# Which engines split the down projection's weights: ScalarE and the Pool in place of the Pool and VectorE

## The chip, the cores and the metric

The kernel runs on one core of one Trainium2 chip. The metric is the device time of one execution in microseconds (us). The profile names the engines PE (TensorE matmul), PEld (TensorE weight load), DVE (VectorE), ACT (ScalarE), POOL (GpSimd) and SP (the engine that issues the DMAs).

## The reference

A two-layer backbone over 1024 latent tokens and 256 context tokens of width 1024, in float32. Layer 0 mixes with chunked gMLP gating beside a bidirectional gated DeltaNet, layer 1 with latent attention; both end in a ConvFFN, which is where the change lies:

```python
def conv_ffn(h, w_up, conv_w, w_down):
    g, u = jnp.split(dwconv(h @ w_up, conv_w), 2, axis=-1)
    return (jax.nn.silu(g) * u) @ w_down

lat = lat + g2 * conv_ffn(modulate(rms_norm(lat, norm2_g[i]), sh2, sc2), ffn_w_up[i], ffn_conv_w[i], ffn_w_down[i])
```

The hidden width is 2816, so `w_down` is 2816 x 1024. Layer 0 runs the ConvFFN over latent and context tokens (1280), layer 1 over the latent ones (1024). A final RMSNorm follows.

## The kernel before, in words

Activations lie transposed: features on the 128 partitions, tokens along the free dimension. Every large product is done in three matmuls on float32r operands. Each operand is split in two halves: `hi` is the value cast to float32r, `lo` is the value minus `hi`, and the product is `hi*hi + hi*lo + lo*hi`. The helper `split(hi, lo, src, eng)` (L130) does this with one cast (`cast`, L119 to L128) and one subtraction (L133); `eng` chooses the engines. With `"pool"` the Pool casts (L126) and DVE subtracts; with `"act"` ACT casts (L124) and DVE subtracts; with `"pools"` the Pool does both.

A ConvFFN has two passes. `ffn_up` multiplies by `w_up`, convolves along the tokens, gates, and stores the 22 hidden tiles in DRAM. `ffn_down` (L544), the second pass, multiplies by `w_down`. It goes over chunks of tokens: in layer 0 one of 512 columns and three of 256, in layer 1 one of 512 and two of 256. For each chunk it computes the output in two halves of four 128-row tiles (`oh`), each half in four PSUM banks. A half needs 11 weight tiles of 128 x 1024 (`wdr`, 512 KB each), so a chunk needs 22, and the tiles are loaded and split anew in every chunk: 22 x 4 + 22 x 3 = 154 times. One weight tile feeds a group of 24 matmuls (L633 with `wdh` and the activation's upper half `ah`, L634 with `wdh` and `al`, L635 with `wdl` and `ah`).

The order of work is kept three tiles deep. After group i is issued, `weight(i + 2)` splits the tile two groups ahead, and `load(i + 3)` asks SP for the raw tile three groups ahead. There are three raw buffers and three pairs of split buffers, so the split of tile i + 2 has to wait until PE has finished group i - 1, and the load of tile i + 3 until the split of tile i has read its raw buffer. `fetch` and `halve` bring the hidden tiles of later groups from DRAM and split them with ACT and DVE (`ah`, `al`). After each half, DVE adds the four PSUM banks, times a gate, onto the residual `x` (L650).

Beside the groups runs the `tail` of a chunk: squares on ACT and the Pool (L206, L208), their sums by matmul (`nsum` L196, `nall` L217), the inverse root on ACT and DVE (L219 to L230), and then in layer 0 the modulation of the eight tiles of the next mixer's input (L249 to L254, two tiles on the Pool by `affine`, L236, six on DVE and ACT) and in layer 1 the final norm (L2128 to L2131). The first steps of a tail run in the chunk's second half, the rest in the first half of the chunk after.

Each engine runs its own queue in order. What goes first in a queue is set by the framework's planner, which orders the instructions by its own model of time when the kernel is built; buffers and semaphores are placed by it as well.

Of the kernel before, what the change touches and what calls it, by code (L numbers as in the profile page):

```python
# [10 lines left out]
ALU = mybir.AluOpType  # L11
# [38 lines left out]
def f(ap):  # L50
    return ap.bitcast(F32)
# [46 lines left out]
class Kern:  # L98
# [30 lines left out]

    def split(self, hi, lo, src, eng):  # L130

        self.cast("pool" if eng == "pools" else eng, hi, src)
        (self.nc.gpsimd if eng == "pools" else self.nc.vector).tensor_tensor(lo, src, f(hi), ALU.subtract)  # L133

    def mm3(self, ps, ws, xs, first=True, last=True):

# [407 lines left out]
    def ffn_down(self, l, wp, chunks, groups, tile_x, x, g2, tail, early=None):  # L544
# [7 lines left out]
        raws, W, A, X = {}, {}, {}, {}  # L552

        def load(i):
            if i < total and i not in raws:
                raws[i] = wp.tile([P, KD, P], F32, tag="wur", name="wdr", bufs=3)
                nc.sync.dma_start(raws[i], self.I["w_down"][l, i // npr % 2, i % npr])

        def weight(i):
            load(i)  # L560
            if i < total and i not in W:

                p, bufs = (wp, 2) if i % 3 < 2 else (self.ffz, 1)
                W[i] = [p.tile([P, KD, P], F32R, tag="wu" + a, name="wd" + a, bufs=bufs) for a in "hl"]
                self.split(*W[i], raws[i], "pool")

        def fetch(ch, gi):

# [35 lines left out]
        def run():  # L604
            load(0)
            weight(0)
            load(1)
            fetch(0, 0)
            fetch(0, 1)
            yield  # L610
            weight(1)
            load(2)
            halve(0, 0)
            halve(0, 1)
            yield
            weight(2)
            load(3)
            todo = sequence()
# [1616 lines left out]
```

## Time and profile before

| what | value |
|---|---|
| time, median of 3 runs | 3243.54 us (3239.95 to 3248.44) |
| time of the profiled execution | 3249.41 us |
| its span | 3247.3 us |
| second pass in layer 0 | about 1452 to 1796 us of the span |
| second pass in layer 1 | about 2970 to 3234 us of the span |
| PE / DVE / POOL / ACT busy | 96% / 67% / 40% / 34% |
| casts of `wdr`, Pool | 154, 189.3 us |
| subtractions for `wdl`, DVE | 154, 199.4 us |

A row of the groups view names the line, engine, operation, what is written and read, the shape and the count; behind the bar stand the busy time and the mean of one in ns; behind the second bar stand the idle time of that engine just before these instructions and what ended most of it. A row of the waits view says who waited for whom, with total, times and the longest, in us. A row of the timeline has the start, the duration, the engine, the line and, in brackets, the idle time ahead of it. A row of the windows view has a stretch of the span, its length, and each engine's busy time with the number of instructions, then the granted PE clock, the DMA engines' share and GB/s. A line can be a helper's: L126 and L133 are the cast and the subtraction of every user of `split`, which is why the tile's name matters.

### The profile page before, as it was taken

Reading aid. Unit: us, or ns where it says so; the run is one execution under the profiler, and the core shown is the slowest. Engines: PE = TensorE matmul, PEld = TensorE weight load, DVE = VectorE, ACT = ScalarE, POOL = GpSimd, SP = SyncE. Lnnn points to the kernel's source line nnn. Section 1 sums busy time; section 2 is a strip of 40 time slices with the busy share of each in tenths; the row PEclk is TensorE's granted clock in tenths of the full one; section 3 lists DMA queues with packets and bytes.
Section 4 is the critical chain, followed back from the end, with each engine's and each line's share of the span. In section 5 each row is a group of like instructions: output and inputs, shape, how many; then the busy total and the mean of one; then the engine's idle time right before and its main releaser. Section 6 shows DMA issues by size and latency. Waiting matters only on the chain. (4 is left out here: it accounts for less than half of the span.)

```text
span 3247.3 us, 48696 instructions
## 1 busy us (share of the span) xinstructions
PE 3106.5 (96%) x19029; PEld 2599.4 (80%) x19029; DVE 2167.6 (67%) x3218; ACT 1105.0 (34%) x2136; POOL 1305.6 (40%) x1181
## 2 busy tenths in 40 slices
PE   7999899998999999999999999999999899999998
PEld 5767777896777788887889778988978787777888
DVE  6333877566875578884477456666666888888455
ACT  5322233333432233340111255555542333333110
POOL 3244323553443354532345232122133566663243
PEclk9999999999999999999999999999999899999999
DMA  7344957753144521244466231000033122225464
GB/s 253 124 140 125 303 144 214 229 171 117 40 141 150 162 97 68 70 154 167 137 222 222 72 110 44 27 22 22 8 117 124 46 78 78 78 79 200 165 198 150
DMA packets 254436, 411.40 MB, mean 127 GB/s; under 512 B 46576, under 2 KB 163520, under 8 KB 254080
## 3 DMA queue, kind: packets, MB, share of 16 engines
q1 hardware_dynamic: 254208, 408.31, 39.3%
q8 instruction: 150, 2.46, 0.3%
q14 instruction: 78, 0.64, 0.1%
HBM read 327.47 MB, written 80.78 MB: 126 GB/s over the span
## 5 line engine op out<-in xcount | busy, mean ns | idle before, releaser
L635 PE MATMUL dn<-ah,wdl 128*128 128x256 f32 (+1 forms) x1232 | 385.1, 318 | 15.4 <-DVE wdl L133 15.4
L633 PE MATMUL dn<-ah,wdh 128*128 128x256 f32 (+1 forms) x1232 | 389.5, 317 | 5.0 <-DVE x L650 4.3
L634 PE MATMUL dn<-al,wdh 128*128 128x256 f32 (+1 forms) x1232 | 387.2, 315 | 0.0
L126 POOL TENSOR_SCALAR wdh<-wdr 128x1024 fp32r<-128x1024 f32 x154 | 189.3, 1230 | 358.4 <-PE dn L634 233.0
L133 DVE TENSOR_TENSOR wdl<-wdr,wdh 128x1024 fp32r<-128x1024 f32 x154 | 199.4, 1301 | 176.3 <-POOL wdh L126 174.2
L635 PEld LDWEIGHTS dn<-ah,wdl 128*128 128x128 f32 x1232 | 234.1, 192 | 34.8 <-DVE wdl L133 18.5
L633 PEld LDWEIGHTS dn<-ah,wdh 128*128 128x128 f32 x1232 | 235.9, 191 | 27.8 <-issue 5.1
L634 PEld LDWEIGHTS dn<-al,wdh 128*128 128x128 f32 x1232 | 235.8, 191 | 15.2
L133 DVE TENSOR_TENSOR wul<-wur,wuh 128x1024 fp32r<-128x1024 f32 x106 | 163.3, 1541 | 97.5 <-POOL wuh L126 97.5
L126 POOL TENSOR_SCALAR wuh<-wur 128x1024 fp32r<-128x1024 f32 x106 | 137.0, 1293 | 222.5 <-PE upc L409 111.6
L1721 POOL TENSOR_SCALAR p<-p,rsm 128x1280 f32<-128x1280 f32 x63 | 84.7, 1345 | 325.9 <-DVE rsm L1714 177.0
L675 DVE SCALAR_TENSOR_TENSOR y<-raw,fconv,y 128x1023 f32<-128x1023 f32 (+1 forms) x132 | 174.1, 1347 | 31.6 <-ACT y L420 31.2
L140 PE MATMUL proj<-hh,wih 128*128 128x512 f32 (+1 forms) x512 | 183.8, 361 | 0.0
L677 DVE SCALAR_TENSOR_TENSOR y<-raw,fconv,y 128x1023 f32<-128x1023 f32 (+1 forms) x132 | 180.1, 1386 | 0.1
L141 PE MATMUL proj<-hl,wih 128*128 128x512 f32 (+1 forms) x512 | 177.8, 348 | 1.0 <-DVE hl L254 1.0
L142 PE MATMUL proj<-hh,wil 128*128 128x512 f32 (+1 forms) x512 | 177.1, 346 | 1.1 <-DVE wil L133 1.1
L427 POOL TENSOR_TENSOR y<-y,y 128x1280 f32<-128x1280 f32 (+1 forms) x42 | 119.8, 2853 | 108.1 <-issue 62.7
L393 POOL TENSOR_TENSOR s<-wur 128x512 f32<-128x512 f32 x42 | 72.7, 1731 | 184.4 <-DMA wur<-in_w_up 129.3
L1703 DVE TENSOR_REDUCE mx<-sc 128x1 f32<-128x512 f32 (+1 forms) x192 | 114.5, 597 | 39.9 <-PE sc L1702 37.9
L420 ACT ACTIVATE y<-raw,fconv 128x1280 f32<-128x1280 f32 (+1 forms) x88 | 110.6, 1259 | 82.0 <-DVE raw L436 75.6
L111 ACT ACTIVATE p<-sc,nmx 128x512 f32<-128x512 f32 (+1 forms) x192 | 116.2, 617 | 49.4 <-DVE nmx L1707 49.2
L124 ACT ACTIVATE ah<-al 128x512 fp32r<-128x512 f32 (+1 forms) x77 | 52.4, 744 | 185.2 <-DMA al<-act 174.9
(544 smaller groups left out, 9351.9 us busy)
## 6 DMA issues: line engine op xcount, KB each, us to landing
wdr<-in_w_down SPq DMA_DIRECT2D x154, 512.0 KB, 3.9
adaw<-in_ada_w SPq DMA_DIRECT2D x96, 512.0 KB, 4.2
wur<-in_w_up SPq DMA_DIRECT2D x88, 512.0 KB, 3.6
al<-act SPq DMA_DIRECT2D x20, 1024.0 KB, 7.6
t<-t SPq DMA_DIRECT2D x20, 768.0 KB, 6.6
act<-y SPq DMA_DIRECT2D x22, 640.0 KB, 3.0
act<-y SPq DMA_DIRECT2D x22, 512.0 KB, 2.6
wir<-in_w_t SPq DMA_DIRECT2D x20, 512.0 KB, 4.6
```

The lines of the kernel that those rows point to most:

```text
L111: self.nc.scalar.activation(out, in_, func, **kw)
L126: nc.gpsimd.tensor_scalar(dst, src, 1.0, 0.0, op0=ALU.mult, op1=ALU.add)
L133: (self.nc.gpsimd if eng == "pools" else self.nc.vector).tensor_tensor(lo, src, f(hi), ALU.subtract)
L140: nc.tensor.matmul(ps, wh, xh, start=first and i == 0, stop=False)
L141: nc.tensor.matmul(ps, wh, xl, start=False, stop=False)
L142: nc.tensor.matmul(ps, wl, xh, start=False, stop=last and i == n - 1)
L427: (nc.gpsimd if ci < FT - 1 else nc.vector).tensor_tensor(y[1], y[0], y[1], ALU.mult)
L633: nc.tensor.matmul(pss[o], wh[:, q, :], ah, start=pr == j == 0, stop=False)
L634: nc.tensor.matmul(pss[o], wh[:, q, :], al, start=False, stop=False)
L635: nc.tensor.matmul(pss[o], wl[:, q, :], ah, start=False, stop=pr == npr - 1 and j == 1)
L675: nc.vector.scalar_tensor_tensor(out=y[:, s0 + 1:e], in0=raw[:, s0:e - 1], scalar=w[:, 0:1], in1=y[:, s0 + 1:e], op0=ALU.mult, op1=ALU.add)
L677: nc.vector.scalar_tensor_tensor(out=y[:, s0:e - 1], in0=raw[:, s0 + 1:e], scalar=w[:, 2:3], in1=y[:, s0:e - 1], op0=ALU.mult, op1=ALU.add)
```

## The change

`split` takes an engine name that may end in "s". The name without it chooses the engine of the cast; the "s" says that the Pool subtracts, and otherwise DVE does. `"pool"`, `"act"` and `"pools"` mean what they meant. `ffn_down` now asks for `"acts"`: for each of the 154 weight tiles ACT casts and the Pool subtracts. The loads, the matmuls, the buffers and everything outside of `weight` are written as before.

```diff
     def split(self, hi, lo, src, eng):
 
-        self.cast("pool" if eng == "pools" else eng, hi, src)
-        (self.nc.gpsimd if eng == "pools" else self.nc.vector).tensor_tensor(lo, src, f(hi), ALU.subtract)
+        self.cast(eng.rstrip("s"), hi, src)
+        (self.nc.gpsimd if eng[-1] == "s" else self.nc.vector).tensor_tensor(lo, src, f(hi), ALU.subtract)
...
                 W[i] = [p.tile([P, KD, P], F32R, tag="wu" + a, name="wd" + a, bufs=bufs) for a in "hl"]
-                self.split(*W[i], raws[i], "pool")
+                self.split(*W[i], raws[i], "acts")
```

## The prediction

> **What bounds the kernel now.** I read the page first: its head, its engine shares and the groups that hold the edited instructions.
>
> ```profile
> span 3247.3 us, 48696 instructions
> PE 3106.5 (96%) x19029; PEld 2599.4 (80%) x19029; DVE 2167.6 (67%) x3218; ACT 1105.0 (34%) x2136; POOL 1305.6 (40%) x1181
> ...
> L635 PE MATMUL dn<-ah,wdl 128*128 128x256 f32 (+1 forms) x1232 | 385.1, 318 | 15.4 <-DVE wdl L133 15.4
> L633 PE MATMUL dn<-ah,wdh 128*128 128x256 f32 (+1 forms) x1232 | 389.5, 317 | 5.0 <-DVE x L650 4.3
> ...
> L126 POOL TENSOR_SCALAR wdh<-wdr 128x1024 fp32r<-128x1024 f32 x154 | 189.3, 1230 | 358.4 <-PE dn L634 233.0
> L133 DVE TENSOR_TENSOR wdl<-wdr,wdh 128x1024 fp32r<-128x1024 f32 x154 | 199.4, 1301 | 176.3 <-POOL wdh L126 174.2
> ```
>
> TensorE (PE) is busy 96% of the span. The edited work, 154 casts and 154 subtractions, is never on its path except where a matmul waits for a weight's lower half: 15.4 us in the whole run. Another 4.3 us are waits for the PSUM evictions (L650), which stand in VectorE's (DVE) queue beside those subtractions. So the most that this change can win is 15.4 + 4.3 = 19.7 us, 0.6%. The waits by layer (first row the first ConvFFN, second row the second one) show where:
>
> ```profile
> PE dn L635 <- DVE wdl L133: 12.4, 10, 2.7
> ...
> PE dn L635 <- DVE wdl L133: 3.0, 1, 3.0
> ```
>
> Next I read the rhythm where nothing disturbs it, in the timeline of the second ConvFFN (256-column chunk):
>
> ```profile
> 3152.05 1.06 POOL L126 TENSOR_SCALAR wdh<-wdr 128x1024 fp32r<-128x1024 f32 x1 [1.79 <-PE dn L634]
> 3154.90 1.06 POOL L126 TENSOR_SCALAR wdh<-wdr 128x1024 fp32r<-128x1024 f32 x1 [1.78 <-PE dn L634]
> ...
> 3153.15 1.23 DVE L133 TENSOR_TENSOR wdl<-wdr,wdh 128x1024 fp32r<-128x1024 f32 x1 [1.63 <-POOL wdh L126]
> ```
>
> One weight comes every 2.85 us, which is one group of 24 matmuls. A cast starts when PE leaves the buffer, two groups (5.7 us) before the weight is needed; it takes 1.06, and the subtraction ends at 3154.38, 2.3 us after the start. So 5.7 - 2.3 = 3.4 us are to spare. At 512 columns a group is about twice as long, and nothing there is near the limit.
>
> Then the chunks of 256 columns, one stretch each (three in the first ConvFFN, two in the second):
>
> ```profile
> core 0: us, PE busy (x) PEld busy (x) DVE busy (x) ACT busy (x) POOL busy (x), PEclk, DMA share, GB/s
> 1582.00:1658.00 76.00, 68.46 (x540) 64.61 (x539) 53.33 (x50) 15.98 (x26) 37.10 (x29) 0.98 0.63 211
> 1658.00:1728.00 70.00, 66.06 (x544) 63.72 (x544) 54.57 (x59) 13.65 (x28) 37.40 (x31) 1.00 0.67 216
> 1728.00:1796.00 68.00, 67.07 (x558) 65.38 (x557) 48.38 (x54) 9.15 (x20) 36.64 (x31) 1.00 0.65 208
> ...
> 3093.00:3171.00 78.00, 72.48 (x560) 68.53 (x559) 48.95 (x48) 9.03 (x16) 33.10 (x28) 0.93 0.60 193
> 3171.00:3234.00 63.00, 62.98 (x536) 61.50 (x538) 35.05 (x36) 4.74 (x12) 25.32 (x24) 1.00 0.54 162
> ```
>
> 22 groups of 2.85 would be 62.7 us; four of the five take 68 to 78. There the previous chunk's norm and modulation run beside the groups, DVE is 63 to 78% busy and ACT 12 to 21%.
>
> **What the Pool and DVE do to each other.** These rows are the start of such a burst, and the same DVE pair a little later:
>
> ```profile
> 1609.03 2.21 POOL L249 TENSOR_TENSOR t<-x,t 128x512 f32<-128x512 f32 x1 [0.62 <-DVE t L230]
> 1611.20 1.50 POOL L126 TENSOR_SCALAR wdh<-wdr 128x1024 fp32r<-128x1024 f32 x1
> ...
> 1610.01 3.23 DVE L252 SCALAR_TENSOR_TENSOR t<-x,gs,t 128x512 f32<-128x512 f32 x2
> 1627.94 1.40 DVE L252 SCALAR_TENSOR_TENSOR t<-x,gs,t 128x512 f32<-128x512 f32 x2
> ```
>
> Two DVE instructions with two SBUF inputs take 1.40 us in one place and 3.23 beside Pool work, and the Pool's cast goes from 1.06 to 1.50. They take turns. So I count the time in which either holds the other off: per weight now 1.06 + 1.23 = 2.29 us.
>
> **The change, part by part.** Removed: 154 Pool casts (189.3 us) and 154 DVE subtractions (199.4 us). Added: 154 ScalarE (ACT) casts and 154 Pool subtractions of the same shape. The rows nearest to them:
>
> ```profile
> L124 ACT ACTIVATE ah<-al 128x1024 fp32r<-128x1024 f32 x22 | 22.1, 1052 | 66.7 <-DMA al<-act 66.7
> ...
> L133 POOL TENSOR_TENSOR wkl<-wur,wkh x4: 2438/2806/2842, 2397.0 to 2410.3; 128x1024 fp32r<-128x1024 f32 x4
> ...
> 2397.02 8.37 POOL L133 TENSOR_TENSOR wkl<-wur,wkh 128x1024 fp32r<-128x1024 f32 x3
> 2410.35 2.44 POOL L133 TENSOR_TENSOR wkl<-wur,wkh 128x1024 fp32r<-128x1024 f32 x1
> ...
> L133 DVE TENSOR_TENSOR ol<-o,oh x24: 407/553/2868, 2393.9 to 2417.0; 128x256 fp32r<-128x256 f32 x16, 128x512 fp32r<-128x512 f32 x8
> ```
>
> The cast is the very same instruction form on ACT: 1.05 us each, 162 us in all. The subtraction is the same form on the Pool: 2.44 us at best, 2.81 when DVE's two-input work (ol, up to 2.87 us instead of some 0.6) alternates with it. I take 2.44 for most and 2.81 inside bursts, 154 times, 376 to 432 us against 189 now.
>
> The Trainium skill, "SBUF — State Buffer", section "SBUF: two separate sides", calls the pair of ports that DVE and GpSimd share an exclusive lock held for the whole instruction; the rows above agree (ol 2.87 us beside wkl). "Perfetto Trace Analysis", section "Optimizing Scalar/DVE Operations", draws from it that moving work between these two engines might not help: by that rule alone the sum would be 0, and mine differs only by waits with other causes.
>
> Held time per weight becomes 2.44, against 2.29: the casts leave the contest, the subtraction comes back twice as long. So a burst that is limited by the two engines taking turns stays as long as it is, and I win nothing of the waits inside bursts. What changes is who queues:
>
> (a) DVE's queue gets 22 x 1.3 = 29 us shorter per chunk. Of the 4.3 us of eviction waits about half stood behind subtractions: -2 (bounds -4.3 and 0).
>
> (b) Two waits have a cause that the change removes.
>
> ```profile
> 1456.31 1.18 POOL L126 TENSOR_SCALAR wdh<-wdr 128x1024 fp32r<-128x1024 f32 x1 [4.34 <-issue]
> ...
> 1464.34 1.21 DVE L133 TENSOR_TENSOR wdl<-wdr,wdh 128x1024 fp32r<-128x1024 f32 x1
> ...
> 3124.51 5.54 POOL L2129 TENSOR_TENSOR x<-x,t 128x512 f32<-128x512 f32 x3 [0.68 <-DVE t L230]
> 3130.02 4.39 POOL L126 TENSOR_SCALAR wdh<-wdr 128x1024 fp32r<-128x1024 f32 x3
> ```
>
> At the start of the first ConvFFN's second pass a cast ended at 1457.5 and its subtraction came at 1464.34, behind conv taps on DVE; the Pool is free there: -2 of that wait of up to 2.7 (0 at worst, as activations' halves stay on DVE). At 3124 three Pool products held up the casts for 5.5 us and PE then stood 3.0 us; the cast now goes on ACT meanwhile, and the subtraction ends near 3130.0 + 2.4 = 3132.5 instead of after 3135: -3.
>
> (c) Each weight is ready later: 1.05 + 2.44 = 3.5 us after release instead of 2.3, spare 5.7 - 3.5 = 2.2. Undisturbed chunks hide that. In a burst whose spare is used up, it costs 1.2 us once; the ten waits of the first ConvFFN fall into about five bursts: +5 (0 if the freed DVE catches up, +12 if each wait pays).
>
> (d) The raw weight's buffer comes free by the subtraction, so its reload is issued 1.2 us later.
>
> ```profile
> SPq L557 <- DVE wdl L133: 254.2, 83, 8.5
> ...
> POOL wdh L126 <- DMA wdr<-in_w_down: 48.7, 24, 5.5
> ```
>
> Loads wait for the subtraction 83 times, and 24 casts already waited for a load. Most are hidden by the spare; I charge one, +1 (up to +4 for the longest stretch).
>
> (e) ACT's 162 us lie in an engine that is 34% busy: nothing, unless its order is bad (third rival). Behind a cast that waits for PE's release stand ACT's squares, Ln/Exp and halvings, which have groups of time.
>
> Sum: -2 - 2 - 3 + 5 + 1 = -1 us. The profiled execution took 3249.4 us (span 3247.3 and 2.1 around it), 5.9 above the median of the runs, so its own figure would be 3248; against the median 3243.5 I forecast 3243. Adding the worst and best of the terms gives -9.3 (-4.3 - 2 - 3) to +13 (-3 + 12 + 4), 3234 to 3257 with no burst cured.
>
> **The rivals.**
>
> First, faster: DVE's queue, not the turn-taking, is the cause of the waits. For it: DVE is the busiest engine after PE in the bursts, and in the row at 1464.34 the subtraction alone is late. Against it: held time per weight doesn't fall. It would take nearly all of the 19.7 us away, say 18: 3225.
>
> Second, slower: the Pool becomes the bound of the 256-column chunks. In the first three of them its work beside the weights is
>
> ```profile
> L126 POOL TENSOR_SCALAR wdh<-wdr 128x1024 fp32r<-128x1024 f32 x64 | 84.8, 1327 | 87.9 <-DMA wdr<-in_w_down 38.8 <-PE dn L634 29.7 <-DVE al L133 6.4
> ```
>
> 37.1 + 37.4 + 36.6 - 84.8 = 26.3, or 8.8 us a chunk, 0.40 a group. So it decides once a subtraction takes over 2.85 - 0.40 = 2.45 us on average: right at the best row, below the median of 2.81. At 2.81 a chunk lasts at least 22 x 2.81 + 8.8 = 70.6. Against it: four chunks last 68 to 78 already. For it: today's lateness comes in bursts and partly from loads, and would be added: half of 5 x (70.6 - 62.7) = 39.5, so +20: 3263. The Trainium skill, "GPSIMD Engine Reference", section "Performance versus the Vector engine", has 4497 ns for such an operation on 2048 elements; half of that, an estimate of 2.25 us, would stay under the 2.45, and this rival would fall. This case's own rows, 2.44 and more, are longer and keep it alive.
>
> Third, slower too: ACT's queue. It runs in order, and these waits stand in it:
>
> ```profile
> ACT t L111 <- DVE t L219: 46.8, 4, 15.6
> ```
>
> A cast planned behind such a wait is late by what exceeds 2.2 us. The planner puts ready casts first, which speaks against it; three bad ones of 5 us would be +15: 3258.
>
> That the change doesn't do what it says has no room here: it is one argument and one branch, used nowhere else.
>
> **How the numbers follow.** What a measurement of this kernel can tell from no change is about 0.3%, 9.7 us. Forecast 0.50 (own range 3234 to 3257, of which 0.03 lies above 3253), DVE's queue 0.27, Pool 0.15, ACT 0.08. That the planner orders all engines anew by its own timing widens each by a few us. Faster by over 0.3%: 0.27; within: 0.47; slower: 0.03 + 0.15 + 0.08 = 0.26. The range reaches to the rivals' values, 3226 to 3262.
>
> **What would show it.** Forecast right: L635's idle before it stays at 8 to 18 us and is now put down to the Pool's wdl, which measures 2.4 to 2.8; L650's waits fall to about 2; DVE busy falls by some 200 us, Pool rises by 190 or more. The second rival shows as Pool near 90% in the chunks and idle before L635 over 25; the first as idle before L635 under 4; the third as casts on ACT that wait for other ACT work. A time below 3234 or above 3253 would prove the sum wrong.

## The result, and the profile after

The changed kernel takes 3272.33 us (median of 4 runs, 3269.12 to 3275.48), the kernel before 3242.14 us beside it (4 runs, 3239.95 to 3248.44). The ratio is 1.0087, with a 95% interval of 1.0075 to 1.0099: slower by 30 us, and above the forecast range of 3226 to 3262.

The page of the changed kernel, its head, its engine shares and the groups of the second pass:

```profile
span 3270.3 us, 48651 instructions
PE 3109.7 (95%) x19029; PEld 2597.9 (79%) x19029; DVE 2017.2 (62%) x3064; ACT 1261.4 (39%) x2290; POOL 1487.7 (45%) x1181
...
L133 POOL TENSOR_TENSOR wdl<-wdr,wdh 128x1024 fp32r<-128x1024 f32 x154 | 380.8, 2483 | 213.6 <-ACT wdh L124 204.6
L633 PE MATMUL dn<-ah,wdh 128*128 128x256 f32 (+1 forms) x1232 | 381.3, 318 | 11.7 <-ACT wdh L124 6.8
...
L635 PE MATMUL dn<-ah,wdl 128*128 128x256 f32 (+1 forms) x1232 | 357.5, 320 | 20.3 <-POOL wdl L133 20.0
...
L124 ACT ACTIVATE wdh<-wdr 128x1024 fp32r<-128x1024 f32 x154 | 162.1, 1057 | 243.1 <-PE dn L634 138.2
```

The edited instructions cost what was forecast: 1.057 us a cast on ACT, 2.483 us a subtraction on the Pool. But the waits of the matmuls grew: 20.3 us before L635 (15.4 before the change) and 11.7 before L633 (5.0), the latter mostly for casts. VectorE is busy only 150 us less, though subtractions of 199.4 us have left it. So its other work got some 50 us longer.

Where the time lies is read from windows, one for each second pass, from its first group's first matmul to its last group's last one (in the first ConvFFN to the last group's first one, some 3 us sooner, in every kernel alike). The first fence is the kernel before (first ConvFFN, second ConvFFN), the second the changed kernel:

```profile
1452.80:1792.20 339.40, 324.50 (x2168) 294.08 (x2167) 214.54 (x215) 54.65 (x95) 138.31 (x112) 0.99 0.58 191
2970.20:3233.70 263.50, 257.96 (x1621) 229.72 (x1619) 142.59 (x141) 36.52 (x60) 85.74 (x75) 0.98 0.57 184
```

```profile
1458.20:1807.80 349.60, 329.74 (x2167) 296.31 (x2166) 132.98 (x125) 143.40 (x183) 239.18 (x114) 0.98 0.57 185
2985.70:3256.50 270.80, 258.71 (x1622) 229.36 (x1621) 78.56 (x77) 103.14 (x126) 166.64 (x75) 0.99 0.56 179
```

The two passes together went from 602.9 to 620.4 us: +17.5 of the 23.0 by which the spans differ (the profiled execution of before, 3249.41 us, was itself 7.3 us above the median of its runs, so the runs' 30 show as 23). PE's busy time in them rose from 582.5 to 588.4, so idle time makes +11.5 and slower matmuls +6.0. Most of the rest, 5.4 us, came ahead of the first ConvFFN's second pass (1458.2 against 1452.8). What stands before it moved by 0 to 6 us in one kernel or another; that part is not explained here.

Inside the passes the loss has a clear place. Six groups of the 512-column chunk, the fourth to the ninth, in the kernel before (first ConvFFN, second one) and then in the changed kernel:

```profile
1476.60:1509.60 33.00, 33.00 (x145) 27.02 (x144) 12.20 (x10) 2.01 (x2) 6.51 (x6) 1.00 0.75 259
2986.80:3020.20 33.40, 33.40 (x146) 27.11 (x145) 13.56 (x12) 2.01 (x2) 6.64 (x7) 1.00 0.73 255
```

```profile
1478.00:1519.70 41.70, 36.41 (x145) 28.72 (x145) 12.52 (x6) 8.36 (x8) 21.63 (x8) 0.92 0.64 216
3002.20:3042.10 39.90, 35.34 (x145) 27.99 (x144) 12.17 (x9) 8.24 (x8) 15.15 (x6) 0.96 0.60 201
```

PE had no idle time there before and now stands about 5 us in each, with a granted clock of 0.92 and 0.96: +8.7 and +6.5 us, in the very chunk of which the prediction said that nothing is near its limit. The chunks of 256 columns hardly changed in sum (356.1 us before, 361.7 after). That this sum hides two large moves of opposite sign came out only by the experiments.

### The profile page after: what moved, and what is told of

It reads as the page before. It is cut to its first block, busy times and chain, and to the rows that moved or that the text cites. A ratio compares the mean times of both kernels' runs of the same rounds, so it can differ in the third digit from the quotient of the medians.

```text
span 3270.3 us, 48651 instructions
## 1 busy us (share of the span) xinstructions
PE 3109.7 (95%) x19029; PEld 2597.9 (79%) x19029; DVE 2017.2 (62%) x3064; ACT 1261.4 (39%) x2290; POOL 1487.7 (45%) x1181
## 5 line engine op out<-in xcount | busy, mean ns | idle before, releaser
L133 POOL TENSOR_TENSOR wdl<-wdr,wdh 128x1024 fp32r<-128x1024 f32 x154 | 380.8, 2483 | 213.6 <-ACT wdh L124 204.6
L633 PE MATMUL dn<-ah,wdh 128*128 128x256 f32 (+1 forms) x1232 | 381.3, 318 | 11.7 <-ACT wdh L124 6.8
L634 PE MATMUL dn<-al,wdh 128*128 128x256 f32 (+1 forms) x1232 | 379.9, 316 | 0.0
L635 PE MATMUL dn<-ah,wdl 128*128 128x256 f32 (+1 forms) x1232 | 357.5, 320 | 20.3 <-POOL wdl L133 20.0
L633 PEld LDWEIGHTS dn<-ah,wdh 128*128 128x128 f32 x1232 | 236.7, 192 | 34.3 <-ACT wdh L124 9.3
L635 PEld LDWEIGHTS dn<-ah,wdl 128*128 128x128 f32 x1232 | 221.7, 192 | 43.4 <-POOL wdl L133 25.8
L124 ACT ACTIVATE wdh<-wdr 128x1024 fp32r<-128x1024 f32 x154 | 162.1, 1057 | 243.1 <-PE dn L634 138.2
L133 DVE TENSOR_TENSOR al<-al,ah 128x512 fp32r<-128x512 f32 (+1 forms) x77 | 87.2, 1179 | 133.0 <-ACT ah L124 133.0
```

The costliest lines, as they stand in the source:

```text
L124: nc.scalar.activation(dst, src, AF.Copy)
L133: (self.nc.gpsimd if eng[-1] == "s" else self.nc.vector).tensor_tensor(lo, src, f(hi), ALU.subtract)
L633: nc.tensor.matmul(pss[o], wh[:, q, :], ah, start=pr == j == 0, stop=False)
L634: nc.tensor.matmul(pss[o], wh[:, q, :], al, start=False, stop=False)
L635: nc.tensor.matmul(pss[o], wl[:, q, :], ah, start=False, stop=pr == npr - 1 and j == 1)
```

## The experiments

All were timed against the kernel before on the same chip; edits are against the changed kernel unless said otherwise. After the result I had a first theory: ACT's queue. Casts stand in it behind halvings of activations that wait for a DMA, as in this part of ACT's timeline in the changed kernel:

```profile
1493.45 1.06 ACT L124 ACTIVATE wdh<-wdr 128x1024 fp32r<-128x1024 f32 x1 [6.55 <-DMA wdr<-in_w_down]
...
1504.04 2.01 ACT L124 ACTIVATE ah<-al 128x1024 fp32r<-128x1024 f32 x2 [9.52 <-DMA al<-act]
1508.40 1.06 ACT L124 ACTIVATE wdh<-wdr 128x1024 fp32r<-128x1024 f32 x1 [2.36 <-DMA wdr<-in_w_down]
```

Its rivals: the Pool's long subtraction holds off VectorE, or the Pool's queue is the bound, or the weight is simply ready too late.

### The two halves of the change, one at a time

ACT casts, VectorE subtracts; and: the Pool does both.

```diff
-                self.split(*W[i], raws[i], "acts")
+                self.split(*W[i], raws[i], "act")      # e1_act_dve
+                self.split(*W[i], raws[i], "pools")    # e2_pools
```

> ScalarE casts the weights' upper halves as in the changed kernel, VectorE subtracts for the lower ones as before: the cast's move alone. If ScalarE's queue is the cause (casts stand behind halvings that wait for a DMA), the loss at the starts of the passes stays and the time is 3255 to 3268 us. If the Pool's subtraction is the cause (twice as long, and in turns with VectorE), the loss goes: 3238 to 3248, or below the kernel before.

> The Pool casts and subtracts, ScalarE does neither: the subtraction's move alone, with 1.05 us more on the Pool per weight. If ScalarE's queue is the cause, the time stays within 12 us of the kernel before where weights have spare time, though the Pool's 1.05 + 2.4 = 3.5 us per weight exceed the 2.85 us of a 256-column group: 110 groups x 0.6 = 66 us more at least, 3300 to 3330, all of it in the 256-column chunks and none at the starts of the passes. If the Pool's subtraction is the cause of the present loss at the starts, the first chunks of both layers are long here as well (by 15 us in sum).

Measured: 3228.05 us for ACT with VectorE (ratio to before 0.9954, 0.9942 to 0.9967) and 3351.18 us for the Pool alone (1.0337, 1.0323 to 1.0351). So the change was two moves: **the cast to ACT wins 15 us, the subtraction to the Pool then costs 44**. The page of the run with ACT and VectorE, and its windows of the two passes:

```profile
L633 PE MATMUL dn<-ah,wdh 128*128 128x256 f32 (+1 forms) x1232 | 386.8, 315 | 2.4 <-ACT wdh L124 2.4
L635 PE MATMUL dn<-ah,wdl 128*128 128x256 f32 (+1 forms) x1232 | 382.0, 316 | 4.4 <-DVE wdl L133 4.3
...
L133 DVE TENSOR_TENSOR wdl<-wdr,wdh 128x1024 fp32r<-128x1024 f32 x154 | 192.9, 1255 | 199.8 <-ACT wdh L124 196.8
```

```profile
1455.70:1783.70 328.00, 321.85 (x2168) 293.21 (x2166) 188.32 (x214) 143.66 (x183) 23.98 (x26) 0.99 0.60 199
2961.80:3215.00 253.20, 252.62 (x1621) 225.91 (x1619) 131.38 (x140) 101.69 (x124) 12.83 (x11) 1.00 0.57 192
```

With the same casts in the same ACT queue the matmuls wait 6.8 us instead of 32, and the passes last 581.2 us. Against the changed kernel that is 39.2 us less, 25.3 of it idle time of PE (32.0 against 6.7) and 13.9 faster matmuls (588.4 against 574.5 us busy). The first theory doesn't survive this run. The Pool-alone run was above its expected range of 3300 to 3330. In it the Pool has 1.17 + 2.48 = 3.65 us of work per weight where a group of the 256-column chunks lasts 2.85; there it is the bound, as L635's group on the page of that run shows:

```profile
L635 PE MATMUL dn<-ah,wdl 128*128 128x256 f32 (+1 forms) x1232 | 353.5, 330 | 71.6 <-POOL wdl L133 71.4
```

The six groups are long in this run as well, about 46 and 43 us, though ACT casts no weight: the loss at the starts goes with the Pool's subtraction.

### Halvings off ACT

```diff
-        def halve(ch, gi, eng="act"):
+        def halve(ch, gi, eng="dve"):
```

> The changed kernel, but VectorE casts the upper halves of the activations in the second pass (the halvings), so that no instruction that waits for an activation's DMA stands ahead of a weight's cast on ScalarE. If ScalarE's queue is the cause, the loss at the starts (8.7 us in layer 0, 6.5 in layer 1) goes: 3255 to 3260. If the Pool's subtraction is, the time stays at 3268 to 3276.

Measured: 3283.38 us (1.0127, 1.0113 to 1.0141), 11 us slower than the change and above both expectations. The matmuls' waits before L633 go to 19.9 us, 15.1 of them for the evictions on VectorE (L650). The six groups get shorter, about 37 and 38 us, but the 512-column chunks as a whole do not (261.8 us, 262.2 in the changed kernel). Freeing ACT's queue at VectorE's cost makes the kernel slower, so VectorE is the scarcer engine. With the run above, ACT's queue is not the cause on its own; its waits are links in a chain, as the next sections show.

### Where the 44 us arise

The Pool subtracts only from the second chunk on, or only from the ninth weight on:

```diff
-                self.split(*W[i], raws[i], "acts")
+                self.split(*W[i], raws[i], "pool" if i < 2 * npr else "acts")   # e4_acts_late
+                self.split(*W[i], raws[i], "act" if i < 8 else "acts")          # f5_acts_from_8
```

> The changed kernel, but the first chunk of each pass (512 columns, 22 weights) keeps the Pool's cast and VectorE's subtraction. If the loss sits at the starts of the passes, by ScalarE's queue, 3254 to 3260. If it is the Pool's subtraction in the 256-column chunks, where a group lasts only 2.85 us, 3266 to 3276, as the first chunk has spare time in any case.

> The changed kernel, but the first eight weights of each pass are subtracted by VectorE (cast by ScalarE as all others). Theory now: the Pool's subtractions hold off VectorE's two-input instructions (conv taps, the halvings' subtractions, the last gate product), while the up projection ends; the store of that product stands in SP's queue ahead of the weight loads, so they come late and PE starves around the fourth to the ninth group. Then 3254 to 3261 (15 us back), with groups 3 to 9 as long as in the kernel before. If the loss of the first chunk is ScalarE's cast behind a halving, or the longer subtraction anywhere in the chunk, 3266 to 3276.

Measured: 3257.38 us (1.0043, 1.0029 to 1.0057) and 3257.09 us (1.0043, 1.0031 to 1.0056). Eight weights at the start of each pass hold 15 of the 44 us. With them on VectorE the six groups are as long as ever:

```profile
1477.50:1510.50 33.00, 33.00 (x146) 27.00 (x145) 6.04 (x5) 8.27 (x9) 7.20 (x3) 1.00 0.67 234
```

The mechanism is seen on VectorE, at the end of `ffn_up`, whose last tile is still being convolved and gated while the second pass begins. The changed kernel first, then the run with ACT and VectorE:

```profile
1457.85 6.34 DVE L133 TENSOR_TENSOR al<-al,ah 128x512 fp32r<-128x512 f32 x4
...
1478.36 3.36 DVE L677 SCALAR_TENSOR_TENSOR y<-raw,fconv,y 128x1023 f32<-128x1023 f32 x1
1481.65 2.88 DVE L133 TENSOR_TENSOR al<-al,ah 128x512 fp32r<-128x512 f32 x1
1484.46 3.70 DVE L427 TENSOR_TENSOR y<-y,y 128x1280 f32<-128x1280 f32 x1
```

```profile
1465.42 1.28 DVE L677 SCALAR_TENSOR_TENSOR y<-raw,fconv,y 128x1023 f32<-128x1023 f32 x1
...
1470.47 2.49 DVE L133 TENSOR_TENSOR al<-al,ah 128x512 fp32r<-128x512 f32 x4
...
1476.74 1.48 DVE L427 TENSOR_TENSOR y<-y,y 128x1280 f32<-128x1280 f32 x1
```

Four subtractions of `al` take 6.34 us instead of 2.49, a conv tap 3.36 instead of 1.28, the last gate product 3.70 instead of 1.48. Each of the last two is longer by about 2.1 to 2.2 us, just under one Pool subtraction. The Trainium skill, "SBUF — State Buffer", section "SBUF: two separate sides", says that of a GpSimd operation and a VectorE operation with two SBUF inputs the one that starts first holds the shared ports for the whole instruction; these rows agree.

The product late on VectorE is what the store of the last hidden tile waits for, and the store stands first in SP's queue. That queue in the changed kernel:

```profile
1488.19 0.33 SPq L428 DMA_DIRECT2D act<-y  x1
1488.62 0.37 SPq L557 DMA_DIRECT2D wdr<-in_w_down  x1
...
1492.28 0.65 SPq L571 DMA_DIRECT2D al<-act  x1
```

and its head in the kernel before:

```profile
1479.21 0.33 SPq L428 DMA_DIRECT2D act<-y  x1
1480.34 0.33 SPq L557 DMA_DIRECT2D wdr<-in_w_down  x1
...
1483.12 0.61 SPq L571 DMA_DIRECT2D al<-act  x1
```

Everything behind the store goes out about 9 us later, or 7.6 counted from the fourth group's first matmul (1476.6 before, 1478.0 here): the next weights and the activations of the chunk's later groups. ACT's long waits for `wdr` and `al`, shown at the head of this section, are their landings.

To take the weights out of that line, their loads went to ACT's DMA queue, with the Pool's subtraction and, as a control, with VectorE's:

```diff
-                nc.sync.dma_start(raws[i], self.I["w_down"][l, i // npr % 2, i % npr])
+                nc.scalar.dma_start(raws[i], self.I["w_down"][l, i // npr % 2, i % npr])   # f6_loads_on_act
...
+                self.split(*W[i], raws[i], "act")                                          # f8_act_loads_act: both
```

> The changed kernel with the loads of the down projection's weights issued from ScalarE's queue in place of SP's, so that they do not stand behind the store of the last gate product. If SP's queue is what carries the lateness to PE, most of the 15 us at the starts come back: 3256 to 3264. If the weights are late for another reason (the Pool's queue, the halving that waits for its DMA ahead of a cast), 3268 to 3280.

> ScalarE casts, VectorE subtracts, and the loads of the down projection's weights go out from ScalarE's queue. With no Pool subtraction there is no late store, so SP's queue has nothing to lose there: 3224 to 3232, as with the cast's move alone. If SP's queue still delays loads, 3215 to 3223.

Measured: 3260.92 us (1.0051, 1.0038 to 1.0064), 11 of the 15 us back; and 3229.39 us (0.9953, 0.994 to 0.9967), no clear difference from the 3228.05 with the loads on SP. So the late store reaches the matmuls mostly by the queue of loads, and only where the Pool's subtraction makes it late. The activations' fetches were still behind it: in the first of the two runs a halving on ACT waits 9.68 us for `al` (until 1503.64), ahead of the ninth group's cast.

### What the remaining 29 us are

They lie in the 256-column chunks. Counted from the start of each chunk's first matmul to the end of its last, these took 356.1 us before, 361.7 in the changed kernel and 333.9 with ACT and VectorE. Three explanations were left: the Pool's own queue, VectorE held off, a weight that is ready later.

**The Pool's queue.** The two tiles of the modulation and the three of the final norm, which the Pool does beside the groups, went to VectorE and ACT; the Pool kept its squares:

```diff
-POOLK = (1, 4, 7)
+POOLK = ()
...
-            if k in (1,4):
+            if k in (1,4) and not steps:
```

> The changed kernel with the chunks' modulation and final norm taken off the Pool (VectorE and ScalarE do these tiles as well; two of eight squares stay). If the 256-column chunks lose by the Pool's own queue (subtractions stand behind the tail's products there), the part of the loss in these chunks falls by 8 us or more: 3256 to 3264. If they lose by the Pool and VectorE taking turns, or because a weight is simply ready later, the work has only moved to the other of the two and the time stays at 3267 to 3280.

Measured: 3270.85 us (1.0088, 1.0074 to 1.0101), the same as the change. A stretch of 145 us in these chunks, the changed kernel and then this one:

```profile
1655.00:1800.00 145.00, 136.09 (x1105) 129.82 (x1104) 64.24 (x68) 70.75 (x98) 121.58 (x62) 1.00 0.68 217
```

```profile
1655.00:1800.00 145.00, 139.32 (x1130) 134.13 (x1129) 60.02 (x78) 70.55 (x99) 115.21 (x50) 0.99 0.67 214
```

The Pool has 12 instructions less there (50 against 62), but the 256-column chunks together are no shorter (364.7 us, 361.7 in the changed kernel). By itself that shows little, since the work went to VectorE, and 115.21 of 145 us on the Pool are left. The changed kernel's trace says more. In its 256-column chunks PE stands for more than 0.25 us in 15 groups. In 11 of them the Pool itself had been idle for 0.97 us or more just before the subtraction, because the cast came late. In only two (subtractions at 1704.39 and 3147.3) did it stand behind one of the Pool's own products. So the Pool's queue is not what bounds these chunks.

Why the casts come late is seen in one of those groups, in the changed kernel:

```profile
1696.92 2.57 POOL L133 TENSOR_TENSOR wdl<-wdr,wdh 128x1024 fp32r<-128x1024 f32 x1
1697.15 2.63 DVE L252 SCALAR_TENSOR_TENSOR t<-x,gs,t 128x256 f32<-128x256 f32 x1
1699.81 0.51 ACT L253 ACTIVATE h0h<-t,mv 128x256 fp32r<-128x256 f32 x1 [3.68 <-DVE t L252]
...
1701.35 2.39 POOL L133 TENSOR_TENSOR wdl<-wdr,wdh 128x1024 fp32r<-128x1024 f32 x1 [0.97 <-ACT wdh L124]
1703.80 0.39 PE L635 MATMUL dn<-ah,wdl 128*128 128x256 f32 x1 [0.59 <-POOL wdl L133]
```

VectorE's modulation product (L252), 0.47 us at its shortest, starts behind a Pool subtraction and takes 2.63, until just after the subtraction ends. ACT waits for that product, and the next weight's cast stands behind it, at 1700.23; so that weight's subtraction and the matmuls come late too. In 5 of the 15 groups the cast is late behind such a product, in 4 behind a halving, in 4 because the raw tile landed late.

**The length of the Pool's instruction.** The Pool subtracts one half of the tile, VectorE the other:

```diff
-                self.split(*W[i], raws[i], "acts")
+                self.cast("act", W[i][0], raws[i])
+                for e, k in ((self.nc.gpsimd, 0), (self.nc.vector, 4)):
+                    e.tensor_tensor(W[i][1][:, k:k + 4], raws[i][:, k:k + 4], f(W[i][0][:, k:k + 4]), ALU.subtract)
```

> The changed kernel, but the Pool subtracts four of a weight's eight slices and VectorE the other four: the Pool's part is halved (2.4 to about 1.2 us), and the two parts can not be long. If the cost follows the length of the Pool's subtraction (how long it holds VectorE off, and how late the weight is), about half of the 44 us between the cast's move alone (3228) and the changed kernel (3272) is left: 3240 to 3256. If any Pool instruction of two inputs costs as much by its mere presence, 3264 to 3276.

Measured: 3241.23 us (0.9995, 0.9987 to 1.0004). Some 13 of the 44 us are left, less than half. The Pool's part took 1.740 us in the mean, not 1.2, since it meets VectorE's part of the same tile; the length fell by 30%, not by half. And the weight is also ready sooner, so this run does not tell the two apart.

**Later without the Pool, and the Pool without being later.** In the first run ACT casts, then writes one more, unsubtracted copy into the lower half's tile, and then VectorE subtracts: the lower half is ready and the raw buffer free as late as with the Pool. In the second ACT and VectorE do the work, and the Pool repeats the subtraction into the raw tile afterwards, which nothing reads.

```diff
-                self.split(*W[i], raws[i], "acts")
+                self.cast("act", W[i][0], raws[i])                                         # h1_late_only
+                self.cast("act", W[i][1], raws[i])
+                nc.vector.tensor_tensor(W[i][1], raws[i], f(W[i][0]), ALU.subtract)
...
+                self.split(*W[i], raws[i], "act")                                          # h2_ports_only
+                nc.gpsimd.tensor_tensor(raws[i], raws[i], f(W[i][0]), ALU.subtract)
```

> ScalarE casts as in the run with the VectorE subtraction (3228 us), then ScalarE writes the lower half's tile once with an unsubtracted copy (1.06 us, later overwritten), and only then VectorE subtracts. So the lower half is ready and the raw buffer free about 1.06 + 1.06 + 1.25 = 3.4 us after release, as with the Pool's subtraction (1.06 + 2.44 = 3.5), while the Pool does nothing for the weights. Lateness theory (of the 29 us that the Pool's subtraction costs in the 256-column chunks, most is the later weight and the later reload): 3250 to 3260. Turn-taking theory (VectorE's two-input instructions are held off by the Pool's long one): 3226 to 3234, idle time before L635 under 8 us.

> ScalarE casts and VectorE subtracts as in the run of 3228 us; behind VectorE's subtraction the Pool does the same subtraction once more, into the raw tile, which nothing reads afterwards. So the lower half is ready as early as in that run, and the Pool holds what it shares with VectorE for the same 2.44 us per weight as in the changed kernel; the raw buffer comes free later still (about 1.06 + 1.25 + 2.44 = 4.75 us after release). Turn-taking theory: as bad as the changed kernel or a little worse, since VectorE's own 1.25 us come on top: 3268 to 3285. Lateness theory with the weight as the late one: 3228 to 3240. If the late raw buffer alone is the cause, this run and the one with the late copy are both slow, and the matmuls' waits in this one lead over casts that wait for a DMA.

Measured: 3238.61 us (0.9989, 0.9981 to 0.9998) and 3337.94 us (1.0294, 1.0279 to 1.0309). Both lie outside what either theory expected (of the first, only the idle time before the weight's last matmuls, 6.0 us, is as turn-taking had it). Lateness alone, with ACT's 154 extra copies, costs 11 us over the run with ACT and VectorE. That is a real part, a quarter of the 44, and it adds to the 15 at the starts of the passes, since the six groups take 33.0 us in this run too. The Pool's repeated subtraction costs 110. Its page:

```profile
L566 POOL TENSOR_TENSOR wdr<-wdr,wdh 128x1024 f32<-128x1024 f32 x154 | 411.9, 2682 | 253.4 <-DVE wdl L133 244.0
L636 PE MATMUL dn<-ah,wdl 128*128 128x256 f32 (+1 forms) x1232 | 368.9, 328 | 55.9 <-DVE wdl L133 55.7
...
L133 DVE TENSOR_TENSOR wdl<-wdr,wdh 128x1024 fp32r<-128x1024 f32 x154 | 285.7, 1864 | 158.3 <-ACT wdh L124 153.3
L124 ACT ACTIVATE wdh<-wdr 128x1024 fp32r<-128x1024 f32 x154 | 162.0, 1056 | 291.7 <-DMA wdr<-in_w_down 159.4
```

VectorE's subtraction grows from 1.255 to 1.864 us although nothing in front of it changed, and L635 of the original (here L636) waits 55.9 us for it. The raw tile is also free later than in any other run (casts idle 159.4 us for a load), so the 110 is not held-off time alone.

What VectorE suffers in the chunks is seen in the modulation product (L252), whose shape is the same in every kernel. The kernel before, the changed kernel, the run with ACT and VectorE, and the run that is only late, in this order:

```profile
L252 DVE SCALAR_TENSOR_TENSOR t<-x,gs,t 128x256 f32<-128x256 f32 x18 | 15.7, 892 | 0.8 <-POOL h2l L236 0.6
```

```profile
L252 DVE SCALAR_TENSOR_TENSOR t<-x,gs,t 128x256 f32<-128x256 f32 x14 | 20.5, 1492 | 7.1 <-POOL h0l L236 3.8 <-POOL h2l L236 3.1
```

```profile
L252 DVE SCALAR_TENSOR_TENSOR t<-x,gs,t 128x256 f32<-128x256 f32 x18 | 11.1, 647 | 0.9 <-POOL h2l L236 0.6
```

```profile
L252 DVE SCALAR_TENSOR_TENSOR t<-x,gs,t 128x256 f32<-128x256 f32 x18 | 12.0, 699 | 0.9 <-POOL h2l L236 0.6
```

892 ns beside the Pool's casts, 1492 beside its subtractions, 647 and 699 without either. In the half-and-half run it is 889 ns. One product is only a sample: in the run without the Pool's modulation it is 561 ns, and others are long there. So here is an estimate over all of VectorE's instructions in the 256-column chunks: what each takes above the undisturbed duration of its form (the fastest twentieth in all traces), summed. It is 46 us before, 63 in the changed kernel, 53 without the Pool's modulation, 18 with ACT and VectorE and 16 in the run that is only late. The last one's chunks take 343.0 us: of the 27.8 us between 333.9 and 361.7, lateness without the Pool makes 9.1.

### The cast off the Pool in both passes

The cast's 15 us pointed further. In `ffn_up` the weights were still cast by the Pool and subtracted by VectorE:

```diff
-                self.split(*W[half], raws[ci, half], "pool")
+                self.split(*W[half], raws[ci, half], "act")
...
-                self.split(*W[i], raws[i], "acts")
+                self.split(*W[i], raws[i], "act")
```

> ScalarE casts and VectorE subtracts in both passes of the ConvFFN (in the first pass in place of the Pool's cast): does the gain of the cast's move carry over? If taking a cast out of the turns between the Pool and VectorE is what gave 15 us in the second pass, 106 casts fewer there give a few us more: 3215 to 3226. If ScalarE's queue in the first pass (conv taps' scaling, copies out of PSUM, the sums' casts) is too full, 3232 to 3250.

Measured: 3205.8 us (0.9884, 0.987 to 0.9897), 38 us faster than before and 22 faster than with the second pass alone, and better than the range that was expected. The first pass has 88 such casts, not 106. Its page:

```profile
span 3204.1 us, 48723 instructions
PE 3088.0 (96%) x19029; PEld 2590.3 (81%) x19029; DVE 2103.9 (66%) x3218; ACT 1348.2 (42%) x2378; POOL 1016.6 (32%) x939
```

18 us of it lie between the two second passes, where the second ConvFFN's first pass is: 1175.0 us from the last matmul of the one to the first of the other before, 1156.9 here. This version beats both kernels.

## Why the prediction was wrong

The sum, by medians: the cast's move -15; the subtraction's move +44, of which 15 at the starts of the passes (run with the first eight on VectorE), 11 for lateness (run with the late copy), and 18 or so left over, which needs the Pool at work. That the last part is VectorE held off fits the rows at 1697, L252 and the estimate over all of VectorE's instructions; no run isolates it, since none has the Pool at work on something that is no weight. The parts were also measured in different kernels, whose queues are ordered anew each time.

**The ceiling of 19.7 us** counted only PE's idle time before L633 and L635. The cast alone won 15 in the median and 21.7 in the windows of the passes (602.9 to 581.2): 13.7 idle and 8.0 of busy time (the profiled execution of before lay above its median). The busy time was missing from the ceiling.

**Held time, "I win nothing of the waits inside bursts": the step that failed.** 2.29 us now and 2.44 after were added up as if it didn't matter who holds and how long one instruction is. It failed in both directions. The one-input cast on the Pool was not cheap company: without it L635's idle fell from 15.4 to 4.4 and L252 from 892 to 647 ns. (The casts also leave the Pool's queue, where some stood behind its own products, as at 3124.51; no run tells these two reliefs apart.) And a single 2.4 us instruction is worse than a 1.06 and a 1.23 one: a two-input instruction of VectorE that comes at a bad moment can stand nearly its whole length (3.36 us instead of 1.28, 2.63 instead of 0.47), and VectorE has many of them (the conv taps, gate products, `al` subtractions, modulation). The prediction charged the contest to the weights alone, so the subtraction's move came out at nothing inside bursts; it measured 44 us, of which lateness, the one part that had a term, made 11.

**The prices** were right: 1.05 against 1.057 us for the cast, 2.44 to 2.81 against a mean of 2.483 for the subtraction.

**(a)** The eviction waits were to fall by 2. They stayed (4.3 us before, waits of 2.88 and 1.56 us after), and the wait before L633 as a whole rose from 5.0 to 11.7 us, mostly for casts, a wait that the term didn't have.

**(b)** "The Pool is free there" was true and the wrong question. The Pool had the time, VectorE did not: this is where the 15 us arose, where -2 had been booked. The first three groups did go 4.0 us faster in the first ConvFFN; the next six lost 8.7. The -3 of the second ConvFFN was won only in the runs with VectorE's subtraction: the eleven groups behind the stall (from 3131.6 in the kernel before) are 5.5 us shorter there and 0.2 in the changed kernel.

**(c)** "Undisturbed chunks hide that", and of 512 columns that "nothing there is near the limit", was wrong by the SP queue: a store held up by VectorE held up the loads behind it. As a size, lateness was put at +5 (0 to +12), and the late copy measured 11 (with ACT's extra copies in it): inside the bounds.

**(d)** was not separated from (c); the late copy holds both.

**(e)** ACT at no cost: right as a price. In the run with ACT and VectorE it does the same 154 casts and all is faster. In the changed kernel ACT's order passes VectorE's lateness on to the casts.

**The rivals.** The third (ACT's order) falls with that run as a cause of its own. The second (the Pool as bound, 3263) came nearest in size, but its mechanism is not what happened: the Pool was busy 121.6 of 145 us, 84%, taking its modulation and norm away changed nothing, and it had mostly been idle just before the late subtractions. It is what happens when the Pool casts as well, at 3351. The first (VectorE's queue is the cause, 3225) was right about the scarce engine and wrong about the remedy: VectorE was relieved by taking the cast from the Pool, not by giving the Pool the subtraction.

**What would show it.** Of the marks that were named, L635's idle of 20.3 lay between "8 to 18" and "over 25", and Pool busy rose by 182, a little less than the 190 that was named. The telling one was VectorE: -150 us where -200 was named. The missing 50 us were its other instructions, longer.

## What to carry to other kernels

Before work with two SBUF inputs goes to the Pool, ask what VectorE does meanwhile: how long one Pool instruction is, how many two-input VectorE instructions can meet it, and what waits for the last of those, casts on ACT and stores in the queue of the loads included. Take a one-input cast off the Pool to ACT where ACT has time: here this alone was worth 15 us in one pass and 38 in both, though the Pool was only 40% busy. A change that moves two things at once is worth timing one by one, even if the sum looks like nothing.

## What the runs showed of the hardware that was not expected

A short stall costs more than its length. PE's timeline in the changed kernel, and the windows around it:

```profile
1507.55 0.39 PE L635 MATMUL dn<-ah,wdl 128*128 128x512 f32 x1
1509.51 0.50 PE L633 MATMUL dn<-ah,wdh 128*128 128x512 f32 x1 [1.57 <-ACT wdh L124]
...
1511.95 0.80 PE L635 MATMUL dn<-ah,wdl 128*128 128x512 f32 x1 [1.70 <-POOL wdl L133]
1512.54 0.63 PE L633 MATMUL dn<-ah,wdh 128*128 128x512 f32 x1
```

```profile
1506.00:1512.00 6.00, 2.73 (x12) 1.64 (x10) 1.49 (x2) 3.21 (x4) 2.47 (x2) 0.90 0.47 185
1512.00:1516.00 4.00, 4.00 (x10) 3.13 (x11) 0.00 (x0) 0.00 (x0) 4.00 (x2) 0.50 0.57 153
```

Two waits of 1.57 and 1.70 us, and then the granted clock is 0.50 until about 1517.6, and a matmul takes 0.63 us instead of 0.39. Stretches like this are a part of the slower matmuls counted above, 13.9 of the 39.2 us between the changed kernel and the run with ACT and VectorE. The Trainium skill, "TensorE: Matmul & The Clock Gate", section "HAM oscillation — how this bites in real kernels", warns of idle gaps of more than about 3.4 us; here two gaps of half that length, 2.4 us apart, were enough. In the kernel before, a single wait of 2.99 us (until 3135.5) was enough: from 3136 to 3141 the granted clock was 0.50. It isn't a matter of length alone: in the changed kernel a wait of 2.10 us until 3150.16 and one of 1.56 us until 3153.89 were followed by a granted clock of 1.00.

The second surprise is the size of the last run: the same 154 Pool subtractions, done after the weights are ready and used by nobody, slow the kernel by 110 us, more than twice what they cost when they produce the weights. In that run VectorE's subtractions come on top and the raw tiles come free later, so the 110 has more than one cause.
